# Scores of a gated recurrence in strips of 32 keys, and its values in native float32

## The chip, the cores and the metric

One core of a Trainium2 chip runs the whole program. The metric is the device time of one execution in microseconds; the time before is the median of three runs.

## What is computed

Two layers of a bidirectional encoder over 512 tokens of width 1024. Each layer mixes three branches (latent attention, a gated recurrence, windowed attention) by gates, then adds cross-attention and a SwiGLU block. The change concerns the recurrence, which for each of 8 heads is, forward and once more on reversed time:

```
b = cumsum(log_f)            # within chunks
scores = (q * exp(b)) @ (k * exp(-b)).T     # tril
o = scores @ v + (q * exp(b)) @ state
state = state * exp(b_last) + (k * exp(b_last - b)).T @ v
```

Each head has keys of 128 and values of 64 elements. The sum of both directions is normalized and gated.

## The kernel before

All activations stand transposed, features on the 128 partitions and the 512 tokens along the columns. Weights stream from HBM in 764 blocks of 128x512 float32. Each is split into a high part `whi` (L120, ScalarE, rounded to the reduced format float32r) and a low part `wlo` (L121, VectorE, the rest), and a projection is three matmuls in parts (`mm3`: high x high, high x low, low x high). All matmuls go through `mm` (L151). `split` (L180 on ScalarE, L181 on VectorE) makes such parts of activations.

The recurrence isn't computed as a scan over a state. `hgrn_decay` makes from the gates the decayed queries and keys of one head and direction, once for tokens within 32 (`qk`: forward queries and keys in 0 and 1, backward in 2 and 3), and for four levels of distance the factors `lf` (forward) and `lr` (backward): level 0 for neighbouring 32s, level 1 for neighbouring 64s, levels 2 and 3 for 128s and 256s. `hgrn_scores` then builds the full 512x512 table of scores of the head, keys on partitions, 128 keys at a time:

- bank `bd` gets, for each of the four 128-token blocks `j`, one 128x128 float32 matmul of the forward `qk`, and bank `bb` one of the backward `qk`; 24 small matmuls then overwrite the places in `bd` that lie across 32s and 64s;
- two predicated copies (L482) take the valid places of both banks to `zz`, whose other places stay zero from a memset at the start; an add (L484) sums them; ScalarE (L487) and VectorE (L488) write high and low part into the diagonal blocks of `ah` and `al`;
- eight wide float32 matmuls, in three banks `g`, fill the blocks off the diagonal, which `split` writes into `ah` and `al`.

The values of the head are 12 matmuls in parts of 512 columns (four blocks, three each); the token-major values `vs` come in parts from `vturn`, for two heads at once, and the half of the result that is the other head's is left unread. The loop in `hgrn` goes over 8 heads: scores of head i, projections of head i + 2, values of head i, decay of head i + 2. The order of instructions on each engine is made by the framework's scheduler, not by the source alone. TensorE runs through the projections meanwhile; the code draws buffers from the pools `c8` (14 of 128x2048 float32), `t2` (25 of 128x512) and 8 PSUM banks.

The layers' other parts are unchanged. The latent attention has a token-major copy of its values of its own (`vtoken`, float32 without parts) and multiplies them as half-width float32 matmuls: two heads side by side on the two halves of the array's columns.

Of the kernel before, what the change touches and what calls it, by code (L numbers as in the profile page):

```python
# [48 lines left out]
def _consts():  # L49
    c = np.zeros((P, CTOT), np.float32)  # L50
    inv = (10000.0 ** (-np.arange(16, dtype=np.float32) / np.float32(16))).astype(np.float32)
    ang = np.arange(T, dtype=np.float32)[:, None] * inv[None, :]
    cos = np.cos(ang).T.astype(np.float32)
    sin = np.sin(ang).T.astype(np.float32)
    cs = np.concatenate([cos, cos, -sin, sin], 0)
    one = np.ones((64, T), np.float32)
    rope = np.stack([np.concatenate([one, cs], 0), np.concatenate([cs, one], 0)])
    t = np.arange(T)
    c[:, C_M:C_M + T] = (t % 16 != 0)
    c[:, C_ID:C_ID + P] = np.eye(P)  # L60
    p = np.arange(P)
    c[:, C_SWAP:C_SWAP + P] = (p[:, None] == p[None, :]) | (p[:, None] == (p[None, :] ^ 32))
    c[:, C_BONE:C_BONE + P] = ((p[:, None] // 64) == (p[None, :] // 64))
    j = np.arange(16)
    for i in range(4):
        n = 1 << i
        c[:, C_SM + 16 * i:C_SM + 16 * i + 16] = (j % n != 0)
        c[:, C_SM + 64 + 16 * (3 - i):C_SM + 80 + 16 * (3 - i)] = (j % n != 0)
    same = (p[:, None] // 32) == (p[None, :] // 32)
    mf = (~same) | (p[:, None] <= p[None, :])  # L70
    mb = same & (p[:, None] >= p[None, :])
    m = np.concatenate([mf, mb], 1).astype(np.int32)
    return c, m, rope


class _K:
# [119 lines left out]
    def setup(self):  # L196
        nc = self.nc
        self.cst = self.tl("cst", [P, CTOT])
        nc.sync.dma_start(self.cst, self.cstd)
        self.ident = self.cst[:, C_ID:C_ID + P]  # L200
        nc.vector.memset(self.ones, 1.0)
        nc.vector.memset(self.eps, EPS)

        b = self.vec[:, V_LB:V_LB + 32].rearrange("p (d l h) -> p d l h", d=2, l=2)
        lbt = self.lbt
        v3 = lambda i: lbt[:, i].rearrange("p (d h) -> p d h", d=2)
        mx, e0, e1, s = v3(0), v3(1), v3(2), v3(3)
        tt = nc.vector.tensor_tensor
        tt(mx, b[:, :, 0], b[:, :, 1], op=ALU.max)
        tt(e0, b[:, :, 0], mx, op=ALU.subtract)  # L210
        tt(e1, b[:, :, 1], mx, op=ALU.subtract)
        nc.scalar.activation(lbt[:, 1:3], lbt[:, 1:3], AF.Exp)
        tt(s, e0, e1, op=ALU.add)
        nc.vector.reciprocal(lbt[:, 3], lbt[:, 3])
        tt(e0, e0, s, op=ALU.mult)
        tt(e1, e1, s, op=ALU.mult)
        tt(lbt[:, 4], lbt[:, 1], lbt[:, 1], op=ALU.subtract)
        tt(lbt[:, 5], lbt[:, 1], lbt[:, 2], op=ALU.add)
        tt(lbt[:, 5], lbt[:, 5], lbt[:, 1], op=ALU.subtract)
        nc.vector.tensor_scalar(lbt[:, 6:8], lbt[:, 4:6], -1.0, 1.0, op0=ALU.mult, op1=ALU.add)  # L220

        self.zz = self.tl("zz", [P, 2, 4, P])
        nc.gpsimd.memset(self.zz, 0.0)

    def col(self, c):
        return self.vec[:, c:c + 1]
# [53 lines left out]
    def vturn(self, vf):  # L280

        nc = self.nc
        tb = self.bank([P, 4, P])
        for j in range(4):
            nc.tensor.transpose(tb[:, j], vf[:, j * P:(j + 1) * P], self.ident)
        v = (self.t2(F32R, (P, 4, P)), self.t2(F32R, (P, 4, P)))
        self.split(v[0], v[1], tb)
        return v

    def hgrn(self, l, x, xg, acc):  # L290
# [48 lines left out]
        for i in range(8):  # L339
            pr = i // 2  # L340
            if i > 0:
                a = self.hgrn_scores(heads[i])
            if i % 2 == 0:
                osb = self.t2()
                if 0 < i < 6:
                    values(pr + 1)
            else:
                g = proj("g", pr)
                sg = self.t2()
                last = nc.scalar.activation(sg, g, AF.Sigmoid)  # L350
                if i == 7:
                    self.pin(last)
                nc.vector.tensor_tensor(sg, g, sg, op=ALU.mult)
            if i < 6:
                take_z(heads[i + 2], [proj("f", i + 2), proj("b", i + 2)])
            elif i == 6:
                pre = self.mla_pre(l, h)
                for nm in ("ckv0", "ckv1", "key"):
                    pre[nm]()
            else:  # L360
                for nm in ("cq0", "nckv", "cq1", "rope"):
                    pre[nm]()
            ob = self.bank()
            vh, vl = vs[pr]
            for j in range(4):
                s = slice(j * T, (j + 1) * T)
                self.mm3(ob, (vh[:, j], vl[:, j]), (a[0][:, s], a[1][:, s]), j == 0, j == 3)
            hf = slice(64 * (i % 2), 64 * (i % 2) + 64)
            nc.scalar.activation(osb[hf], ob[hf], AF.Copy)
            if i % 2 == 1:  # L370
                sq = self.t2()
                nc.scalar.activation(sq, osb, AF.Square)
            if i < 6:
                take_q(heads[i + 2], proj("q", i + 2))
                if i % 2 == 0:
                    vs[pr + 1] = self.vturn(st["vf"])
            elif i == 7:
                pre["cq2"]()
            if i % 2 == 1:
                ob = self.bank()  # L380
                self.mm(ob, self.cst[:, C_BONE:C_BONE + P], sq, True, True)
            if i < 6:
                decay(heads[i + 2])
            elif i == 7:
                pre["ncq"]()
            if i % 2 == 1:
                r = self.t2()
                self.rsqrt(r, ob, 64)
                nc.vector.scalar_tensor_tensor(r, osb, self.col(lv + V_GOUT), r, op0=ALU.mult, op1=ALU.mult)
                nc.vector.tensor_tensor(r, r, sg, op=ALU.mult)  # L390
                self.split(y[pr][0], y[pr][1], r)
# [68 lines left out]
    def hgrn_scores(self, hd):  # L460
# [2 lines left out]
        tt = nc.vector.tensor_tensor  # L463
        one = lambda o, a, b: self.mm(o, a, b, True, True)
        qk, lf, lr = hd["qk"], hd["lt", 0], hd["lt", 1]
        bd, bb = self.bank([P, 4, P]), self.bank([P, 4, P])
        for j in range(4):
            js = slice(j * P, (j + 1) * P)
            one(bd[:, j], qk[:, 1, js], qk[:, 0, js])
            one(bb[:, j], qk[:, 3, js], qk[:, 2, js])  # L470
        for j in range(4):
            one(bd[0:64, j, 64:128], lf[:, 1, 1, 64 * j:64 * j + 64], lf[:, 1, 0, 64 * j:64 * j + 64])
            one(bd[64:128, j, 0:64], lr[:, 1, 1, 64 * j:64 * j + 64], lr[:, 1, 0, 64 * j:64 * j + 64])
            for i in range(2):
                a, b = 64 * i, 64 * i + 32
                ps = slice(64 * j + 32 * i, 64 * j + 32 * i + 32)
                one(bd[a:a + 32, j, b:b + 32], lf[:, 0, 1, ps], lf[:, 0, 0, ps])
                one(bd[b:b + 32, j, a:a + 32], lr[:, 0, 1, ps], lr[:, 0, 0, ps])
        ah, al = self.c8([P, 4 * T], F32R), self.c8([P, 4 * T], F32R)
        z = self.zz  # L480
        for i, b in enumerate((bd, bb)):
            nc.vector.copy_predicated(z[:, i], self.msk[:, i].unsqueeze(1).to_broadcast([P, 4, P]), b)  # L482
        zd = self.t2(shape=(P, 4, P))
        tt(zd, z[:, 0], z[:, 1], op=ALU.add)  # L484
        dg = lambda a: bass.AP(a.tensor, a.offset, [list(a.ap[0]), [640, 4], [1, P]])
        dh, dl = dg(ah), dg(al)
        nc.scalar.activation(dh, zd, AF.Copy)  # L487
        tt(dl, zd, dh.bitcast(F32), op=ALU.subtract)  # L488
        h0, h1 = slice(0, P), slice(P, 2 * P)
        for i in range(3):  # L490
            g = self.bank()
# [7 lines left out]
            else:  # L499
                one(g[:, 0:128], lf[:, 2, 1, h1], lf[:, 2, 0, h1])  # L500
                one(g[:, 128:384], lr[:, 3, 1, h1], lr[:, 3, 0])
                one(g[:, 384:512], lr[:, 2, 1, h1], lr[:, 2, 0, h1])
            s = slice(i * 640 + 128, (i + 1) * 640)
            self.split(ah[:, s], al[:, s], g)
        return ah, al

    def branch(self, l, gate, wname, rows, y, h, merged, first):

# [81 lines left out]
    def mla(self, l):  # L590
# [56 lines left out]
                    nc.vector.tensor_copy(pt[:, :, js], tb)  # L647
            return pt

        def vtoken(vf):  # L650

            tb = self.bank([P, 4, P])
            for j in range(4):
                nc.tensor.transpose(tb[:, j], vf[:, j * P:(j + 1) * P], self.ident)
            v = self.t2(shape=(P, 4, P))
            nc.scalar.activation(v, tb, AF.Copy)
            return v

        def values(pr, v, pts):

            def run():
# [8 lines left out]
        self.fill()  # L670
        vf = keys(0)
        self.fill()
        v = vtoken(vf)
        cq = self.mst["n", "cq"]
        qt = query(0)
        self.fill()
# [2 lines left out]
        for hd in range(8):  # L679
# [10 lines left out]
            if e == 1:  # L690
                pend, pts = values(pr, v, pts), []
                if hd < 7:
                    v = vtoken(vf)
            if hd < 7:
                ps = scores(qt, 1 - e)
        return y, pend
# [449 lines left out]
```

## Time and profile before

| what | value |
| --- | --- |
| time, median of 3 runs | 2477.17 us (2470.8 to 2479.98) |
| the profiled execution's own time | 2471.43 us |
| its span | 2469.6 us |
| mean granted TensorE clock | 0.995 |
| TensorE / weight loads / VectorE / ScalarE / GpSimd busy | 98% / 81% / 63% / 49% / 11% |
| recurrence of layer 0, layer 1 in the trace | about 30 to 320 us, 1255 to 1545 us |

Busy time is that of instructions on an engine; a matmul's end is modelled, and matmuls overlap. L151 is line 151 of the kernel, where all matmuls are recorded, so their groups are told apart by tile and shape. 128*64 means 128 rows and 64 columns of the array.

### The profile page before, as it was taken

What the parts mean: (1) busy time and instruction counts of PE and PEld (TensorE: products, weight loads), DVE (VectorE), ACT (ScalarE), POOL (GpSimd) and SP (SyncE); (2) the same over time, 40 slices, a digit from 0 to 9 for tenths busy, and PEclk for the clock granted to TensorE, in tenths of its full rate; (3) what the DMA queues carried; (4) which work ended last, traced back from release to release, by engine and by line L of the source; (5) the groups of instructions that cost most, each with busy time, mean ns of one, the idle gap of its engine ahead of it and who ended that gap; (6) DMA issues with size and microseconds to landing.
All of it is one profiled execution on the core that took longest, in us unless ns stands there. A gap on an engine that the chain in (4) does not pass through costs nothing.

```text
span 2469.6 us, 32711 instructions
## 1 busy us (share of the span) xinstructions
PE 2422.0 (98%) x12038; PEld 1999.7 (81%) x12038; DVE 1545.8 (63%) x2787; ACT 1215.4 (49%) x2213; POOL 262.6 (11%) x197
## 2 busy tenths in 40 slices
PE   8999999999999999999998999999999999999998
PEld 6788877788888888888877887887888888888886
DVE  8888666676665655355577776766766656553553
ACT  7666565455554533233466665654554445332332
POOL 2455300000000000000035542000000000000000
PEclk9999999999999999999999999999999999999999
DMA  4211322223453333333421222221224523333332
GB/s 140 70 61 55 90 74 60 63 73 100 140 138 98 86 95 98 96 96 98 129 73 60 69 74 63 73 64 60 81 79 149 146 78 89 97 96 98 98 96 76
DMA packets 119681, 220.96 MB, mean 89 GB/s; under 512 B 13281, under 2 KB 15585, under 8 KB 119137
## 3 DMA queue, kind: packets, MB, share of 16 engines
q1 hardware_dynamic: 119520, 218.88, 30.1%
q8 instruction: 94, 1.54, 0.3%
q14 instruction: 67, 0.54, 0.1%
HBM read 214.63 MB, written 4.19 MB: 89 GB/s over the span
## 4 chain that ended last, share of the span: by engine, by line
PE 82%; DVE 8%; issue 4%; ACT 3%; POOL 2%; DMA 1%; SPq 0%; DVEq 0%; ACTq 0%; POOLq 0%
PE ps L151 80%; POOL t L404 2%; DVE c L457 1%; PE ps L643 1%; DVE smx L411 1%; ACT whi L120 1%; POOL t L408 1%; DVE c L439 1%; DVE t L411 1%; DVE wlo L121 1%; PE ps L787 0%; DVE c L438 0%; DVE zz L482 0%; DMA c<-in_memT_dram 0%; DVE t L434 0%
## 5 line engine op out<-in xcount | busy, mean ns | idle before, releaser
L151 PE MATMUL ps<-c,whi 128*128 128x512 f32 (+1 forms) x5696 | 1734.7, 386 | 6.2 <-ACT whi L120 6.0
L151 PEld LDWEIGHTS ps<-c,whi 128*128 128x128 f32 x5696 | 1061.0, 188 | 227.7 <-issue 10.8
L151 PE MATMUL ps<-c,wlo 128*128 128x512 f32 (+1 forms) x2848 | 1098.9, 386 | 15.3 <-DVE wlo L121 15.2
L120 ACT ACTIVATE whi<-wraw 128x512 fp32r<-128x512 f32 x764 | 475.2, 630 | 841.7 <-PE ps L151 621.6
L121 DVE TENSOR_TENSOR wlo<-wraw,whi 128x512 fp32r<-128x512 f32 x764 | 520.2, 690 | 533.9 <-ACT whi L120 516.6
L151 PEld LDWEIGHTS ps<-c,wlo 128*128 128x128 f32 x2848 | 536.4, 188 | 126.7 <-DVE wlo L121 20.2
L151 PE MATMUL ps<-c,t 128*128 128x512 f32 (+4 forms) x896 | 185.6, 386 | 4.3 <-DVE c L181 2.8
L404 POOL TENSOR_SCALAR t<-t 128x512 f32<-128x512 f32 x32 | 71.7, 2242 | 1081.2 <-ACT t L401 1079.7
L151 PEld LDWEIGHTS ps<-c,t 128*128 128x128 f32 (+2 forms) x896 | 133.9, 182 | 43.6 <-issue 16.9
L457 POOL TENSOR_TENSOR c<-c,smx 128x256 f32<-128x256 f32 x128 | 145.0, 1161 | 74.3 <-DVE c L438 64.3
L966 DVE TENSOR_TENSOR t<-ps,t 128x512 f32<-128x512 f32 x112 | 76.2, 688 | 103.1 <-PE ps L151 103.1
L180 ACT ACTIVATE c<-ps 128x512 fp32r<-128x512 f32 (+3 forms) x200 | 97.7, 527 | 84.1 <-PE ps L151 81.3
L181 DVE TENSOR_TENSOR c<-ps,c 128x512 fp32r<-128x512 f32 (+3 forms) x200 | 114.9, 598 | 28.5 <-ACT c L180 27.4
L151 PE MATMUL ps<-c 128*32 128x32 f32 (+3 forms) x1280 | 108.1, 255 | 5.5 <-DVE c L439 5.5
L151 PEld LDWEIGHTS ps<-c 128*32 128x32 f32 (+2 forms) x1280 | 94.9, 148 | 21.3 <-DVE c L439 4.0
L948 DVE TENSOR_TENSOR c<-ps,c 128x512 f32<-128x512 f32 x64 | 44.2, 690 | 73.0 <-PE ps L151 73.0
L457 DVE TENSOR_TENSOR c<-c,smx 128x256 f32<-128x256 f32 x128 | 67.7, 587 | 0.3
L181 DVE TENSOR_TENSOR c<-t,c 128x512 fp32r<-128x512 f32 (+1 forms) x84 | 51.9, 633 | 2.9 <-ACT c L180 2.9
L408 POOL TENSOR_TENSOR t<-t,t 128x512 f32<-128x512 f32 x32 | 44.7, 1397 | 84.1 <-ACT t L407 84.1
L180 ACT ACTIVATE c<-t 128x512 fp32r<-128x512 f32 (+1 forms) x84 | 47.8, 581 | 9.4 <-DVE t L390 3.3
L406 ACT ACTIVATE t<-t 128x512 f32<-128x512 f32 x32 | 20.1, 629 | 62.4 <-POOL t L404 62.4
L411 DVE TENSOR_TENSOR_SCAN t<-cst,t 128x512 f32<-128x512 f32 x32 | 40.8, 1275 | 15.8 <-POOL t L408 15.8
(144 smaller groups left out, 1888.7 us busy)
## 6 DMA issues: line engine op xcount, KB each, us to landing
wraw<-in_w_dram SPq DMA_DIRECT2D x764, 256.0 KB, 2.7
c<-in_xT_dram SPq DMA_DIRECT2D x16, 256.0 KB, 5.1
t<-in_bias_dram SPq DMA_DIRECT2D x16, 192.0 KB, 2.8
c<-in_memT_dram SPq DMA_DIRECT2D x3, 1024.0 KB, 8.0
xs<-c SPq DMA_DIRECT2D x8, 256.0 KB, 2.4
c<-xs SPq DMA_DIRECT2D x8, 256.0 KB, 4.3
out_dram<-t SPq DMA_DIRECT2D x8, 256.0 KB, 2.0
t<-in_rope_dram SPq DMA_DIRECT2D x4, 256.0 KB, 3.1
```

The lines of the kernel that those rows point to most:

```text
L120: self.nc.scalar.activation(hi, raw, AF.Copy)
L121: self.nc.vector.tensor_tensor(lo, raw, hi.bitcast(F32), op=ALU.subtract)
L151: self.nc.tensor.matmul(o, a, b, start=start, stop=stop)
L180: nc.scalar.activation(hi, src, AF.Copy)
L181: nc.vector.tensor_tensor(lo, src, hi.bitcast(F32), op=ALU.subtract)
L404: nc.gpsimd.tensor_scalar(g, f, TINY, KNEE, op0=ALU.max, op1=ALU.min)
L408: nc.gpsimd.tensor_tensor(f, f, g, op=ALU.add)
L411: scan = lambda o, m, x: nc.vector.tensor_tensor_scan(o, m, x, 0.0, op0=ALU.mult, op1=ALU.add)
L439: nc.vector.scalar_tensor_tensor(ki, kk, omlb, cc, op0=ALU.mult, op1=ALU.mult)
L457: eng.tensor_tensor(ov, sv, ev, op=ALU.mult)
L948: nc.vector.tensor_tensor(x[c], b, xold[c], op=ALU.add)
L966: self.nc.vector.tensor_tensor(t, b, r, op=ALU.mult)
```

## The change

`hgrn_scores` computes the scores within 128 tokens as strips: 32 keys at a time on one quarter of the array's columns, for the forward 32s, the backward 32s, the level-0 and the level-1 neighbours, four strips in a row on the four quarters. The backward scores need 32 columns a bank row instead of 128. There are no parts any more: one copy of the diagonal blocks, four adds on 32 partitions each for the backward places, one copy for each bank `g`. `vturn` returns float32 values, and the values of a head are four float32 matmuls on its own half of the columns. `vtoken` was the same as the new `vturn` and goes.

```
-    mb = same & (p[:, None] >= p[None, :])
+    mb = (p[:, None] % 32) >= p[None, :]
...
-        self.zz = self.tl("zz", [P, 2, 4, P])
-        nc.gpsimd.memset(self.zz, 0.0)
+        zz = self.tl("zz", [P, 8, P])
+        nc.gpsimd.memset(zz, 0.0)
+        self.zz, self.zb = zz[:, 0:4], zz[:, 4].rearrange("p (a b) -> p a b", a=4)
...
-        v = (self.t2(F32R, (P, 4, P)), self.t2(F32R, (P, 4, P)))
-        self.split(v[0], v[1], tb)
+        v = self.t2(shape=(P, 4, P))
+        nc.scalar.activation(v, tb, AF.Copy)
...
-            vh, vl = vs[pr]
+            hf = slice(64 * (i % 2), 64 * (i % 2) + 64)
             for j in range(4):
-                s = slice(j * T, (j + 1) * T)
-                self.mm3(ob, (vh[:, j], vl[:, j]), (a[0][:, s], a[1][:, s]), j == 0, j == 3)
-            hf = slice(64 * (i % 2), 64 * (i % 2) + 64)
+                self.mm(ob[hf], vs[pr][:, j, hf], a[:, j * T:(j + 1) * T], j == 0, j == 3)
...
-        bd, bb = self.bank([P, 4, P]), self.bank([P, 4, P])
+        bd, bb = self.bank([P, 4, P]), self.bank([P, 4, 32])
+        q4 = [slice(32 * g, 32 * g + 32) for g in range(4)]
         for j in range(4):
-            js = slice(j * P, (j + 1) * P)
-            one(bd[:, j], qk[:, 1, js], qk[:, 0, js])
-            one(bb[:, j], qk[:, 3, js], qk[:, 2, js])
-        for j in range(4):
-            one(bd[0:64, j, 64:128], lf[:, 1, 1, 64 * j:64 * j + 64], lf[:, 1, 0, 64 * j:64 * j + 64])
-            one(bd[64:128, j, 0:64], lr[:, 1, 1, 64 * j:64 * j + 64], lr[:, 1, 0, 64 * j:64 * j + 64])
-            for i in range(2):
-                a, b = 64 * i, 64 * i + 32
-                ps = slice(64 * j + 32 * i, 64 * j + 32 * i + 32)
-                one(bd[a:a + 32, j, b:b + 32], lf[:, 0, 1, ps], lf[:, 0, 0, ps])
-                one(bd[b:b + 32, j, a:a + 32], lr[:, 0, 1, ps], lr[:, 0, 0, ps])
-        ah, al = self.c8([P, 4 * T], F32R), self.c8([P, 4 * T], F32R)
-        z = self.zz
-        for i, b in enumerate((bd, bb)):
-            nc.vector.copy_predicated(z[:, i], self.msk[:, i].unsqueeze(1).to_broadcast([P, 4, P]), b)
-        zd = self.t2(shape=(P, 4, P))
-        tt(zd, z[:, 0], z[:, 1], op=ALU.add)
-        dg = lambda a: bass.AP(a.tensor, a.offset, [list(a.ap[0]), [640, 4], [1, P]])
-        dh, dl = dg(ah), dg(al)
-        nc.scalar.activation(dh, zd, AF.Copy)
-        tt(dl, zd, dh.bitcast(F32), op=ALU.subtract)
+            js = [slice(j * P + 32 * g, j * P + 32 * g + 32) for g in range(4)]
+            for g in range(4):
+                one(bd[q4[g], j, q4[g]], qk[:, 1, js[g]], qk[:, 0, js[g]])
+            for g in range(4):
+                one(bb[q4[g], j], qk[:, 3, js[g]], qk[:, 2, js[g]])
+            for g in range(4):
+                ps = slice(64 * j + 32 * (g // 2), 64 * j + 32 * (g // 2) + 32)
+                lt = lf if g % 2 == 0 else lr
+                one(bd[q4[g], j, q4[g ^ 1]], lt[:, 0, 1, ps], lt[:, 0, 0, ps])
+            for g in range(4):
+                ks = slice(64 * j + 32 * (g % 2), 64 * j + 32 * (g % 2) + 32)
+                lt = lf if g < 2 else lr
+                cs = slice(64, 128) if g < 2 else slice(0, 64)
+                one(bd[q4[g], j, cs], lt[:, 1, 1, ks], lt[:, 1, 0, 64 * j:64 * j + 64])
+        a = self.c8([P, 4 * T])
+        nc.vector.copy_predicated(self.zz, self.msk[:, 0].unsqueeze(1).to_broadcast([P, 4, P]), bd)
+        nc.vector.copy_predicated(self.zb, self.msk[:, 1, 0:32].unsqueeze(1).to_broadcast([P, 4, 32]), bb)
+        dg = bass.AP(a.tensor, a.offset, [list(a.ap[0]), [640, 4], [1, P]])
+        nc.scalar.activation(dg, self.zz, AF.Copy)
+        for g in range(4):
+            tt(dg[q4[g], :, q4[g]], self.zz[q4[g], :, q4[g]], self.zb[q4[g]], op=ALU.add)
...
-            s = slice(i * 640 + 128, (i + 1) * 640)
-            self.split(ah[:, s], al[:, s], g)
-        return ah, al
+            nc.scalar.activation(a[:, i * 640 + 128:(i + 1) * 640], g, AF.Copy)
+        return a
```

## Rows read from the trace of the kernel before

**Rows 1.** The page: span, and each engine's busy us, share, instructions.

```profile
span 2469.6 us, 32711 instructions
...
PE 2422.0 (98%) x12038; PEld 1999.7 (81%) x12038; DVE 1545.8 (63%) x2787; ACT 1215.4 (49%) x2213; POOL 262.6 (11%) x197
```

**Rows 2.** Busy time by stage: length, PE, PEld, DVE, ACT, POOL, clock, DMA, GB/s.

```profile
30.00:320.00 290.00, 276.89 (x1602) 226.41 (x1601) 221.60 (x404) 183.19 (x308) 130.05 (x96) 0.99 0.23 69
...
620.00:1255.00 635.00, 634.93 (x2946) 530.15 (x2945) 347.44 (x565) 257.59 (x452) 0.00 (x0) 1.00 0.37 107
1255.00:1545.00 290.00, 276.17 (x1595) 225.11 (x1594) 218.62 (x399) 180.75 (x306) 131.37 (x96) 0.98 0.22 68
```

**Rows 3.** Waits of TensorE, 30 to 320 us: total, times, longest.

```profile
PE ps L151 <- DVE wlo L121: 5.8, 4, 2.3
...
PE ps L151 <- DVE c L181: 1.7, 1, 1.7
```

**Rows 4.** Waits of TensorE, 1255 to 1545 us.

```profile
PE ps L151 <- DVE wlo L121: 9.4, 6, 3.7
...
PE ps L151 <- DVE c L181: 1.0, 1, 1.0
```

**Rows 5.** TensorE alone by stretch, one head's scores: length, busy (count), clock, DMA, GB/s.

```profile
123.09:124.96 1.87, 1.87 (x17) 1.00 0.67 149
124.96:126.82 1.86, 1.86 (x49) 1.00 0.37 134
126.82:129.46 2.64, 2.64 (x24) 1.00 0.00 0
...
125.23:125.43 0.20, 0.20 (x12) 1.00 0.89 328
```

**Rows 6.** Timeline of TensorE, one head's values: start, us, instructions.

```profile
147.42 2.88 PE L151 MATMUL ps<-c,t 128*128 128x512 f32 x12
150.14 0.61 PE L151 MATMUL ps<-c,whi 128*128 128x512 f32 x2
```

**Rows 7.** Timeline of TensorE, one pair of attention values and its neighbours.

```profile
375.30 0.39 PE L151 MATMUL ps<-t,wlo 128*128 128x512 f32 x1
375.62 3.65 PE L151 MATMUL ps<-c,t 128*64 128x512 f32 x16
379.20 0.73 PE L151 MATMUL ps<-c,whi 128*128 128x512 f32 x2
```

**Rows 8.** Groups of VectorE instructions, 30 to 320 us: busy, mean ns, idle before.

```profile
L181 DVE TENSOR_TENSOR c<-ps,c 128x512 fp32r<-128x512 f32 x24 | 15.4, 678 | 0.2 <-ACT c L180 0.2
...
L482 DVE COPY_PREDICATED zz<-msk,ps 128x512 f32<-128x512 int32 x16 | 11.7, 735 | 2.6 <-PE ps L151 2.6
...
L434 DVE TENSOR_TENSOR t<-t,smx 128x256 f32<-128x256 f32 x16 | 6.7, 418 | 0.0
L488 DVE TENSOR_TENSOR c<-t,c 128x512 fp32r<-128x512 f32 x8 | 6.6, 831 | 0.0
...
L484 DVE TENSOR_TENSOR t<-zz 128x512 f32<-128x512 f32 x8 | 5.5, 681 | 0.1
...
L425 DVE TENSOR_TENSOR smx<-smx,t 128x64 f32<-128x64 f32 x16 | 4.3, 270 | 0.1
```

**Rows 9.** Timeline of VectorE ahead of a wait of TensorE.

```profile
143.68 0.68 DVE L484 TENSOR_TENSOR t<-zz 128x512 f32<-128x512 f32 x1
144.29 0.68 DVE L121 TENSOR_TENSOR wlo<-wraw,whi 128x512 fp32r<-128x512 f32 x1
```

**Rows 10.** Timeline of TensorE at that wait; in brackets idle and releaser.

```profile
143.16 0.61 PE L151 MATMUL ps<-c,whi 128*128 128x512 f32 x2
145.02 0.50 PE L151 MATMUL ps<-c,wlo 128*128 128x512 f32 x1 [1.24 <-DVE wlo L121]
```

**Rows 11.** Busy time by stretch around a fall of the clock, as rows 2.

```profile
105.40:108.00 2.60, 0.33 (x2) 0.00 (x0) 2.60 (x10) 1.22 (x3) 0.16 (x1) 1.00 0.00 0
108.70:112.00 3.30, 3.30 (x10) 2.49 (x8) 3.27 (x5) 3.29 (x7) 3.25 (x4) 0.50 0.30 79
```

More of the change, by code (lines that the diff above doesn't have):

```diff
@@ L648, in turned @@
             return pt
[L650 to L657, printed above, removed]
         def values(pr, v, pts):
@@ L672, in mla @@
         self.fill()
-        v = vtoken(vf)
+        v = self.vturn(vf)
         cq = self.mst["n", "cq"]
@@ L692, in mla @@
                 if hd < 7:
-                    v = vtoken(vf)
+                    v = self.vturn(vf)
             if hd < 7:
```

## The prediction

> **What bounds the kernel now.** Read first the busy time of each engine over the span: TensorE is busy 2422.0 of 2469.6 us, VectorE 1545.8, ScalarE 1215.4 [rows 1]. So there is hardly a stretch where TensorE could be filled better, and a change pays mainly by making TensorE's own work shorter. Next the same view by stage. The two stretches with the recurrence (30 to 320 us and 1255 to 1545 us) are where TensorE is idle: 290.00 - 276.89 = 13.1 us in the first, 13.8 us in the second; between 620 and 1255 us it is idle for 0.1 us of 635 [rows 2]. In those two stretches VectorE is busy 221.6 and 218.6 of 290 us, three quarters of the time. The view of waits says who was late: the low part of a streamed weight block (`wlo`, L121, a VectorE subtraction) in 4 waits of 5.8 us together in the first stretch and 6 waits of 9.4 us in the second, and the low part of the scores (`c`, L181) in 1.7 and 1.0 us [rows 3, 4]. VectorE is late there, and a TensorE matmul stands behind it. The change edits this stage alone: 8 heads in each of 2 layers, 16 calls of `hgrn_scores`.
>
> **TensorE, scores within 128 tokens.** Now: eight 128x128 float32 matmuls, then 24 small ones. The trace has two MATMUL records for each float32 matmul, so 16 and 48. They take 1.87 and 1.86 us, together 3.73 us a head [rows 5]; a count in these rows includes the records still in flight at its start. (The eight wide matmuls behind them, 2.64 us [rows 5], stay.) New: 16 rounds of four strip matmuls, 32 keys on each quarter of the columns, 12 rounds with 32 queries streamed and 4 with 64; together 64 matmuls, 128 records. No row shows rounds back to back, so I bound them.
>
> Low end: a 128-column record takes 1.87/16 = 0.117 us. A strip loads and streams a quarter of the columns: estimate 0.029 us, and two records in a row on each quarter make a round of 0.058 us, or 0.117 us with 64 queries. Per 128 tokens 3 x 0.058 + 0.117 = 0.29 us, times 4 = 1.17 us. A change of the array's shape costs about 0.09 us: before the attention values the last wide matmul begins at 375.30 and would be followed 0.227 us later (three matmuls of this kind take 0.68 us: 12 in 2.72 [rows 6]), but the first half-width one begins at 375.62 [rows 7]. In and out: 0.18 us. Sum 1.35 us.
>
> High end: four strips with their eight records took 0.20 us, 125.23 to 125.43, to the next shape [rows 5]; they run side by side, or they would take longer than a full 128-column pair. Sixteen such rounds and 4 x 0.058 for the wider ones: 3.43, with 0.09 on the way in 3.5 us.
>
> I take the row that is nearest, four strips, less the change of shape that is in it: 0.20 - 0.09 = 0.11 us a round; 16 x 0.11 + 0.23 + 0.18 = 2.2 us. That saves 3.73 - 2.2 = 1.5 us a head; between 2.4 and 0.2 by the bounds.
>
> The Trainium skill, "TensorE: Matmul & The Clock Gate", section "Back-to-back issue gap", speaks against this: it gives a matmul of 1 to 64 columns a floor of some 60 cycles, about 25 ns, and by that the estimate for 128 records is 3.2 us. The rows neither show nor exclude it: eight records in 0.20 us are 25 ns each, but with the change of shape in them.
>
> **TensorE, values.** Now 12 matmuls of 512 columns in parts, from 147.42 to 150.14: 2.72 us [rows 6]. New: four float32 matmuls, eight records, on 64 columns. The attention values are the same form: 16 records, two halves of the array side by side, run from 375.62 to 379.20, 3.58 us [rows 7]. Here one half is empty, so eight records take as long as those sixteen. With 0.09 us into the shape, and the pair of wide matmuls behind it taking 0.73 instead of 0.62 us, it is 3.78 us: 1.06 us more a head. This term is sure to 0.1 us. The move from parts to native float32 is a loss on TensorE; it is VectorE that gains by it.
>
> TensorE together: -1.5 + 1.06 = -0.47 us a head, -7.5 us for 16; by the bounds -21 to +13 us. Since TensorE is busy almost throughout, I count it in full.
>
> **VectorE.** Per head go: the add L484 (0.681), the subtraction L488 (0.831) and three subtractions at L181 from PSUM (0.678 each) [rows 8]. The second predicated copy (L482, 0.735) shrinks from 512 to 128 columns. Four adds on 32 partitions and 128 columns come; 64 columns cost 0.270 and 256 cost 0.418 [rows 8], so I take 0.31 each, and the same for the short copy. Old 4.28, new 5 x 0.31 = 1.55 us: 2.7 us a head, 43 us in all; the token turn of the values loses its subtraction too. ScalarE keeps its copies, one for each it had.
>
> This is worth only what TensorE waits. Look at one wait: the weight matmul of 143.16 is followed at 145.02, 1.24 us idle, released by L121 [rows 10]; VectorE did the add L484 from 143.68 and only then L121 from 144.29 [rows 9]. Without L484 (0.6 us from start to start) and with the second copy 0.4 us shorter earlier in this chain, L121 comes 1.0 us sooner and 0.2 us of wait is left. Ten such waits hold 15.2 us, two more 2.7 us [rows 3, 4]: at most 18 us, and about 12 us at 1.0 us each. I take 7.5 us. The framework's scheduler orders VectorE anew, one of the four adds can land where L484 was, and a TensorE that is faster by 0.5 us a head comes to the same weight block earlier. What is late next is the decay of the following head, which fills VectorE ahead of L121 and stays. Nothing is counted for the clock: the granted clock was 0.50, the level of 1.2 GHz, from 108.70 to 112.00, right behind 2.60 us in which TensorE was busy for 0.33 [rows 11]; shorter waits there could give back up to half of these 3.3 us.
>
> **Edits costed at nothing.** The memset has the same 1024 columns, at the start, under loading. `zz` and `zb` are read by ScalarE and the four adds until the next head's copies, some 30 us later. One `c8` buffer a head instead of two and one `t2` for the values only free memory. No DMA moves; weights flow as before. The adds wait for ScalarE's copy of the diagonal, since both write it; behind a waiting add on VectorE stand L121 and the next decay. The copy itself no longer waits for L484, so I expect no new stall. If it comes, each costs up to 0.6 us, one ScalarE copy.
>
> **Sum.** -7.5 (TensorE) - 7.5 (waits) = -15 us. The profiled execution took 2471.4 us, so 2456 us in its own terms; it lies 5.7 us under the median of three, 2477.2, whose runs spread over 9 us. In terms of the median: 2462 us.
>
> **Rivals.**
> 1. The strips run at the pace of their columns (1.35 us a block). For it: the four side by side in 0.20 us with a change of shape. Then -21 - 7.5 = -28.5: 2449 us.
> 2. Every record costs 25 ns however narrow, block 3.5 us. The row of four strips has just this pace; against it, the change of shape is inside. Then +13 - 7.5 = +5.5: 2483 us. The floor of the Trainium skill, above, would give a block close to this one.
> 3. Slower: TensorE hands out small records no faster than in the 24 small matmuls, 48 in 1.86 us, 39 ns each. Then the block takes 4.96 us, each head 1.23 + 1.06 = 2.3 us more, +36.6 - 7.5 = +29: 2506 us. It decides beyond half a per cent from 31 ns a record on (block 3.9 us). Against it: seven changes of shape lie in those 1.86 us.
> 4. TensorE as I say, but VectorE's new order keeps L121 as late as it is: -7.5 alone, 2470 us.
>
> **How the numbers follow.** Chances: forecast 0.42, its own range 2453 to 2471; rival 1 0.20, rival 2 0.20, rival 3 0.10, rival 4 0.08. What this kernel's measurement can tell from no change is about half a per cent, 12.4 us, so faster means under 2464.8. Of the forecast 0.26 lies under that and 0.16 over it. Faster: 0.26 + 0.20 = 0.46. Same: 0.16, rival 4 and nearly all of rival 2: 0.42. Slower: rival 3 and the rest, 0.12. A range of 2443 to 2488 us leaves out rival 3 and the outer part of rival 1, some 0.16.
>
> **What would show it.** Right: a head's strip block of 128 records in 2.0 to 2.5 us between the last 128-column projection and the first wide score matmul; eight half-width records of about 0.43 us apart for the values; VectorE some 45 us less busy; waits on L121 in these two stretches down from 15.2 to about half. Wrong: a block over 3 us (rivals 2 and 3) or under 1.6 us (rival 1); waits at the old sum, or a new one on the four adds or on the values' matmuls.

## The result, and the profile after

The changed kernel is 1.1% slower: 2505.24 us median (2502.49 to 2506.14) against 2478.27 us for the kernel before on the same chip, a ratio of 1.0113 [1.009, 1.0135]. Forecast were 2462 us, in a range of 2443 to 2488 us. One execution further down, the profiled one of e8, was disturbed (8207.31 us, where its other six took 2462.73 to 2466.68), and what e8 waits for is read from e12, the same kernel.

The page of the kernel after: span and busy time, beside [rows 1].

```profile
span 2502.9 us, 34617 instructions
...
PE 2419.5 (97%) x12998; PEld 1955.0 (78%) x12998; DVE 1517.1 (61%) x2763; ACT 1220.2 (49%) x2217; POOL 237.8 (10%) x197
```

TensorE is idle for 2502.9 - 2419.5 = 83.4 us; before it was 2469.6 - 2422.0 = 47.6 us. Its busy time hardly fell, but work takes nearly twice the busy time at half the clock (three matmuls of a weight block 1.28 us, 219.53 to 220.81 in the trace after, where they take 0.68 at full clock). The mean granted clock went from 0.995 to 0.987, so the loss to the clock, span times one minus clock, is some 12.3 us before and 32.5 us after (the third digit leaves 1.2 us open in each). What remains is work at full clock: 2422.0 - 12.3 = 2409.7 before, 2419.5 - 32.5 = 2387.0 after. So the 33.3 us of longer span are **-22.7 work, +35.8 idle, +20.2 clock**. This split is used for all runs below. It is a rough one: a part of the low clock falls in the waits themselves, so it books somewhat too much as clock and too little as work. It also holds for one execution of each kernel, and that of before took 2471.43 us, below its median; by the medians the change costs 27.0 us and not 33.3.

Busy time by stage after, as [rows 2]; the two recurrences are now the first and last row.

```profile
30.00:335.00 305.00, 274.27 (x2075) 203.02 (x2074) 205.88 (x391) 184.37 (x308) 118.43 (x96) 0.95 0.21 66
...
620.00:1260.00 640.00, 639.93 (x2977) 534.56 (x2976) 346.61 (x566) 259.00 (x459) 0.00 (x0) 1.00 0.36 109
1260.00:1580.00 320.00, 287.76 (x2131) 213.31 (x2130) 216.16 (x408) 192.28 (x323) 118.25 (x96) 0.96 0.20 63
```

All of it is in the recurrence: 30.7 and 32.2 us idle where it was 13.1 and 13.8, and the clock 0.95 and 0.96 where it was 0.99 and 0.98. Who is waited for, first recurrence and then second, beside [rows 3, 4]:

```profile
PE ps L151 <- DVE wlo L121: 16.8, 4, 5.6
PE ps L151 <- DVE c L489: 7.9, 3, 3.5
...
PE ps L151 <- DVE wlo L121: 19.4, 6, 5.5
PE ps L151 <- DVE c L489: 7.9, 3, 3.5
```

Waits on L121 rose from 15.2 to 36.2 us, with as many waits; new are 15.8 us for the four adds (L489).

**TensorE's own work did fall.** One head's strips after, beside the first two rows of [rows 5], TensorE alone:

```profile
122.83:124.23 1.40, 1.40 (x129) 1.00 0.00 1
```

The block takes 1.40 us where it took 3.73. The values after, beside [rows 6]:

```profile
75.40 0.39 PE L151 MATMUL ps<-c,wlo 128*128 128x512 f32 x1
75.72 3.65 PE L151 MATMUL ps<-c,t 128*64 128x512 f32 x8
79.30 0.73 PE L151 MATMUL ps<-c,whi 128*128 128x512 f32 x2
```

From 75.72 to 79.30 they take 3.58 us where it was 2.72. With the two changes of shape (0.32 us from the last wide matmul into it where 0.23 is usual, and 0.73 for the next pair where 0.62 is) it is 3.78, as forecast. Together -2.33 + 1.06 = -1.27 us a head, -20 us for 16 heads: that is the -22.7 above, within what its rounding leaves open.

**Where it went: a wait of 5.57 us.** It is in the fifth head. TensorE, then VectorE, then GpSimd at this place of the kernel after:

```profile
211.48 0.61 PE L151 MATMUL ps<-c,whi 128*128 128x512 f32 x2
217.66 0.79 PE L151 MATMUL ps<-c,wlo 128*128 128x512 f32 x1 [5.57 <-DVE wlo L121]
```

```profile
199.91 0.75 DVE L484 COPY_PREDICATED zz<-msk,ps 128x512 f32<-128x512 int32 x1
...
211.48 1.10 DVE L389 TENSOR_TENSOR t<-t,t 128x512 f32<-128x512 f32 x1
212.51 2.68 DVE L456 TENSOR_TENSOR c<-c,smx 128x256 f32<-128x256 f32 x4
...
215.72 1.17 DVE L489 TENSOR_TENSOR c<-zz 32x128 f32<-32x128 f32 x4
216.92 3.10 DVE L121 TENSOR_TENSOR wlo<-wraw,whi 128x512 fp32r<-128x512 f32 x5
```

```profile
211.07 3.51 POOL L456 TENSOR_TENSOR c<-c,smx 128x256 f32<-128x256 f32 x4 [1.57 <-ACT whi L120]
```

The same head in the kernel before, in the same order:

```profile
210.05 0.50 PE L151 MATMUL ps<-c,wlo 128*128 128x512 f32 x1 [1.16 <-DVE wlo L121]
```

```profile
194.45 0.75 DVE L482 COPY_PREDICATED zz<-msk,ps 128x512 f32<-128x512 int32 x1
...
206.77 1.42 DVE L457 TENSOR_TENSOR c<-c,smx 128x256 f32<-128x256 f32 x4
...
208.71 0.68 DVE L484 TENSOR_TENSOR t<-zz 128x512 f32<-128x512 f32 x1
209.31 0.68 DVE L121 TENSOR_TENSOR wlo<-wraw,whi 128x512 fp32r<-128x512 f32 x1
```

```profile
205.75 6.90 POOL L457 TENSOR_TENSOR c<-c,smx 128x256 f32<-128x256 f32 x4 [1.70 <-DVE c L438]
```

The chain on VectorE is the same: the predicated copy, the decay of the next head, the gated output of the last pair of heads (L390 before, L389 after), the add or adds, L121. From the copy to L121 it took 209.31 - 194.45 = 14.86 us and now takes 216.92 - 199.91 = 17.01, though one copy has left it: of the rows shown, the four multiplies (L457, now L456) take 1.26 us longer, and the four adds 0.49 us longer than the one add. The wait grew by 5.57 - 1.16 = 4.41 us: 2.15 from this chain, and the other 2.26 is TensorE, which arrives sooner by nearly the 2.33 that the score block lost.

At the place of [rows 9, 10], the third head, on which the forecast worked out its term, VectorE and TensorE after:

```profile
128.98 0.75 DVE L484 COPY_PREDICATED zz<-msk,ps 128x512 f32<-128x512 int32 x1
...
144.78 0.68 DVE L121 TENSOR_TENSOR wlo<-wraw,whi 128x512 fp32r<-128x512 f32 x1
```

```profile
145.51 0.80 PE L151 MATMUL ps<-c,wlo 128*128 128x512 f32 x1 [4.29 <-DVE wlo L121]
```

Here the adds stand behind this L121, and the chain is still 15.80 us long. Before, the copy began at 129.39, so it was 144.29 - 129.39 = 14.90: L121 comes 0.90 us later in the chain, not 1.0 us sooner, and the wait is 4.29 instead of 1.24 us.

Behind the wait of 5.57 us the clock falls, as in [rows 11]:

```profile
212.10:217.60 5.50, 0.00 (x0) 0.00 (x0) 5.43 (x12) 5.36 (x10) 2.48 (x3) 0.91 0.00 0
218.00:223.40 5.40, 5.40 (x12) 3.32 (x12) 2.71 (x5) 1.67 (x4) 0.00 (x0) 0.50 0.73 243
```

The second kind of wait is in the second, fourth and sixth head: the values stand ready and wait for the adds, which VectorE runs behind the same multiplies of the decay. TensorE, then VectorE:

```profile
181.93 5.32 PE L151 MATMUL ps<-c,t 128*64 128x512 f32 x8 [2.21 <-DVE c L489]
```

```profile
178.00 2.69 DVE L456 TENSOR_TENSOR c<-c,smx 128x256 f32<-128x256 f32 x4
180.61 1.16 DVE L489 TENSOR_TENSOR c<-zz 32x128 f32<-32x128 f32 x4
```

### The profile page after: what moved, and what is told of

Same layout as the page of the kernel before. It is cut to its first block, busy times and chain, and to the rows that moved or that the text cites. A ratio compares the mean times of both kernels' runs of the same rounds, so it can differ in the third digit from the quotient of the medians.

```text
span 2502.9 us, 34617 instructions
## 1 busy us (share of the span) xinstructions
PE 2419.5 (97%) x12998; PEld 1955.0 (78%) x12998; DVE 1517.1 (61%) x2763; ACT 1220.2 (49%) x2217; POOL 237.8 (10%) x197
## 4 chain that ended last, share of the span: by engine, by line
PE 79%; DVE 10%; issue 4%; ACT 4%; POOL 3%; DMA 0%; SPq 0%; DVEq 0%; POOLq 0%; ACTq 0%
PE ps L151 77%; DVE c L456 2%; POOL t L403 2%; PE ps L643 1%; DVE smx L410 1%; DVE wlo L121 1%; DVE c L438 1%; DVE t L410 1%; POOL t L407 1%; ACT whi L120 1%; DVE smx L428 1%; DVE c L437 1%; PE ps L778 0%; DVE t L433 0%; DVE c L489 0%
## 5 line engine op out<-in xcount | busy, mean ns | idle before, releaser
L151 PE MATMUL ps<-c,wlo 128*128 128x512 f32 (+1 forms) x2848 | 1102.7, 387 | 36.3 <-DVE wlo L121 36.2
L120 ACT ACTIVATE whi<-wraw 128x512 fp32r<-128x512 f32 x764 | 476.9, 630 | 878.2 <-PE ps L151 655.4
L121 DVE TENSOR_TENSOR wlo<-wraw,whi 128x512 fp32r<-128x512 f32 x764 | 524.5, 695 | 580.5 <-ACT whi L120 559.8
L151 PE MATMUL ps<-c,t 128*64 128x512 f32 (+4 forms) x832 | 202.3, 426 | 17.2 <-DVE c L489 15.8
L151 PEld LDWEIGHTS ps<-c,t 128*128 128x128 f32 (+2 forms) x832 | 115.5, 175 | 87.7 <-issue 48.1
L456 POOL TENSOR_TENSOR c<-c,smx 128x256 f32<-128x256 f32 x128 | 118.5, 955 | 77.0 <-DVE c L437 58.8
L180 ACT ACTIVATE c<-ps 128x256 fp32r<-128x256 f32 (+3 forms) x152 | 72.1, 507 | 71.0 <-PE ps L151 68.6
L181 DVE TENSOR_TENSOR c<-ps,c 128x256 fp32r<-128x256 f32 (+3 forms) x152 | 84.1, 574 | 32.6 <-ACT c L180 31.6
L151 PEld LDWEIGHTS ps<-c 128*32 128x32 f32 (+1 forms) x2304 | 64.9, 124 | 22.0 <-issue 8.0
L151 PE MATMUL ps<-c 128*32 128x32 f32 (+3 forms) x2304 | 74.1, 223 | 7.9 <-DVE c L438 6.3
L456 DVE TENSOR_TENSOR c<-c,smx 128x256 f32<-128x256 f32 x128 | 75.1, 645 | 0.2
L405 ACT ACTIVATE t<-t 128x512 f32<-128x512 f32 x32 | 20.2, 630 | 62.9 <-POOL t L403 62.9
L151 PE MATMUL ps<-t,whi 128*128 128x512 f32 x160 | 49.5, 390 | 0.0
```

The lines of the kernel that those rows point to most:

```text
L120: self.nc.scalar.activation(hi, raw, AF.Copy)
L121: self.nc.vector.tensor_tensor(lo, raw, hi.bitcast(F32), op=ALU.subtract)
L151: self.nc.tensor.matmul(o, a, b, start=start, stop=stop)
L180: nc.scalar.activation(hi, src, AF.Copy)
L181: nc.vector.tensor_tensor(lo, src, hi.bitcast(F32), op=ALU.subtract)
L456: eng.tensor_tensor(ov, sv, ev, op=ALU.mult)
```

## The experiments

Each time is a median, each ratio is to the kernel before on the same chip with its 95% interval; idle and clock are worked out as above from each run's span, TensorE busy time and mean granted clock. The kernel before had medians of 2475.93 to 2479.93 us in its four sets of runs, so a difference between two rows is good to about 4 us.

| run | us | ratio | idle | clock | L121 waits |
| --- | --- | --- | --- | --- | --- |
| before (profiled 2471.4) | 2478.3 | | 47.6 | 12 | 15.2 |
| after | 2505.2 | 1.0113 [1.009, 1.0135] | 83.4 | 33 | 36.2 |
| e1 padded | 2494.4 | 1.0063 [1.0044, 1.0083] | 54.9 | 20 | 23.3 |
| e2 no adds | 2477.7 | 1.0001 [0.9989, 1.0013] | 63.9 | 25 | 31.3 |
| e3 parts earlier | 2506.0 | 1.0108 [1.0087, 1.0128] | 83.1 | 35 | 35.7 |
| e4 scores first | 2436.3 | 0.9829 [0.981, 0.9848] | 36.3 | 10 | 2.6 |
| e5 before, scores first | 2493.5 | 1.0063 [1.0042, 1.0085] | 61.9 | 22 | 2.8 |
| e6 strips only | 2529.9 | 1.0207 [1.0185, 1.0229] | 118.6 | 56 | 82.4 |
| e7 values only | 2488.8 | 1.0034 [1.0021, 1.0047] | 48.7 | 17 | 20.9 |
| e8 strips only, scores first | 2463.7 | 0.9942 [0.9926, 0.9958] | | | |
| e9 scores first, padded | 2482.8 | 1.0019 [1.0003, 1.0036] | 50.4 | 17 | 21.1 |
| e10 scores first, no adds | 2435.2 | 0.9835 [0.982, 0.9849] | 34.0 | 10 | 3.2 |
| e11 values only, scores first | 2463.4 | 0.9949 [0.9934, 0.9963] | 31.1 | 7 | 3.3 |
| e12 as e8, for its trace | 2466.0 | 0.9954 [0.994, 0.9968] | 70.4 | 25 | 14.6 |

**e1, more work for TensorE.** Eight matmuls into a bank that nothing reads, in each head:

```
+        pad = self.bank([P, 4, P])
+        for _ in range(2):
+            for j in range(4):
+                js = slice(j * P, (j + 1) * P)
+                one(pad[:, j], qk[:, 1, js], qk[:, 0, js])
```

> The changed kernel with eight more 128x128 float32 matmuls in every head's score block, into a bank that nobody reads: some 1.9 us more TensorE work a head, 30 us in all, at the place where the strips saved it. Theory A (what the strips and values save on TensorE is not lost there, but turns into waiting: TensorE now comes early to a weight block whose low part, L121, stands behind the next head's decay in VectorE's order): the time stays within 10 us of the changed kernel's 2505, since the waits on L121 and on the adds L489 shrink by about what is added. Theory B (the strips or the half-width values themselves cost the time): 2535 us.

Sixteen records of 0.117 us are 1.87 us a head [rows 5], 30 us in all, and the kernel became 10.8 us faster: 0.8 us outside theory A's range, and 41 us from theory B's time. TensorE and VectorE at the place of the 5.57 us:

```profile
214.06 0.50 PE L151 MATMUL ps<-c,wlo 128*128 128x512 f32 x1 [3.77 <-DVE wlo L121]
```

```profile
208.91 2.69 DVE L456 TENSOR_TENSOR c<-c,smx 128x256 f32<-128x256 f32 x4
...
212.12 1.16 DVE L494 TENSOR_TENSOR c<-zz 32x128 f32<-32x128 f32 x4
213.31 3.10 DVE L121 TENSOR_TENSOR wlo<-wraw,whi 128x512 fp32r<-128x512 f32 x5
```

VectorE's order here is unchanged, and the wait is shorter by 5.57 - 3.77 = 1.80 us, what the padding takes. So at this wait TensorE's shorter block had bought nothing: what it saved it waited, one for one. Over the kernel the waits on L121 fall from 36.2 to 23.3 us and those on the adds (L494 here) from 15.8 to 0.7, 28.0 us together for some 30 us of added work, and the clock gives back some 12.

**e2, without the four adds.**

```
-        for g in range(4):
-            tt(dg[q4[g], :, q4[g]], self.zz[q4[g], :, q4[g]], self.zb[q4[g]], op=ALU.add)
```

> The changed kernel without the four narrow adds L489, so without the backward scores within 32 tokens. Theory C (the adds are the new cost: narrow instructions on VectorE, and TensorE's values waiting for them): back to the kernel before or below it, under 2480 us. Theory A: the adds are 1.2 us of a chain of 17 us; the waits on L489 go (16 us in the trace), but the weight blocks behind the decay are only 1.2 us earlier each; 2485 to 2497 us, waits on L121 still over 25 us.

Theory A's range is missed, theory C's number is met: 27.6 us less than after. The 15.8 us of waits on L489 go, L121 waits 4.9 us less, and the clock gives back some 8. So the four adds, 1.17 us of VectorE's time a head, cost 1.7 us a head. Of the 36.2 us for L121, 31.3 stay.

**e3, weights taken apart earlier.** How many weight blocks ahead L120 and L121 are issued:

```
-LOOK = 3
+LOOK = 4
```

> The changed kernel with the weight parts made one 512-column unit earlier (LOOK 4 instead of 3): VectorE gets L121 some 2.7 us of TensorE work sooner. Theory A: the ten waits on L121 of 36 us lose up to 2.7 us each, and the clock falls less often; 2475 to 2490 us. Theory C (adds): the waits on L489 stay and the time moves by less than 8 us. If the time doesn't move at all, the order of L121 against the decay is not the cause.

No change, and theory A's gain missed. By the expectation's last sentence that speaks against the order as the cause. But the edit didn't move the order. VectorE of e3 at the place of the 5.57 us:

```profile
201.85 0.75 DVE L484 COPY_PREDICATED zz<-msk,ps 128x512 f32<-128x512 int32 x1
...
218.85 3.10 DVE L121 TENSOR_TENSOR wlo<-wraw,whi 128x512 fp32r<-128x512 f32 x5
```

From the copy to L121 it is 17.00 us, where it was 17.01, and the wait is 5.56: one block more of lookahead in the code leaves L121 where it stood, behind the decay. So e3 says nothing for or against the order.

**e4, scores of the next head ahead of the decay.** In the loop over heads:

```
-            if i > 0:
-                a = self.hgrn_scores(heads[i])
...
+            if i < 7:
+                a = self.hgrn_scores(heads[i + 1])
             if i < 6:
                 decay(heads[i + 2])
```

> The changed kernel with each head's scores issued ahead of the decay of the head after it, instead of behind it; the same work. VectorE's order then has the adds and several L121 between the pieces of the decay. Theory A: waits on L489 nearly go (16 us to under 4) and those on L121 halve; 2450 to 2475 us, under the kernel before, since the TensorE work that was saved (some 22 us) can then be had. Theory B: no better than 2495 us.

The whole loss is gone and 42 us of the time before with it, 14 us more than theory A's best. VectorE, ahead of the place where TensorE waited:

```profile
127.32 1.17 DVE L489 TENSOR_TENSOR c<-zz 32x128 f32<-32x128 f32 x4 [0.52 <-ACT c L487]
...
135.81 0.66 DVE L121 TENSOR_TENSOR wlo<-wraw,whi 128x512 fp32r<-128x512 f32 x1
...
140.22 1.12 DVE L121 TENSOR_TENSOR wlo<-wraw,whi 128x512 fp32r<-128x512 f32 x1
141.26 2.68 DVE L456 TENSOR_TENSOR c<-c,smx 128x256 f32<-128x256 f32 x4
```

The adds come in the middle of the decay, and L121 is let in ahead of its last multiplies. The multiplies themselves take as long as after at this place, and longer over the whole kernel (87.3 us for VectorE's 128, against 75.1); VectorE is as busy (1514.0 us). No wait on L489 is left, and 2.6 us on L121. The same work in another order is worth 69 us. The edit moves the scores on every engine, so this is the worth of the whole order and not of VectorE's alone.

**e5, the same move in the kernel before.** The diff is that of e4 on the old code.

> The kernel before, with each head's scores issued ahead of the decay of the head after it: the same move as in the run with scores first, without the change. Theory A (order on VectorE and the change are two things that add up): it wins what the kernel before waits for VectorE and the slow clock behind it, 10 to 20 us: 2458 to 2468 us, so that in this order the change is worth 20 to 30 us. Theory D (the order only mends what the change broke): 2478 us, within 6.

Both forecasts missed: some 15 us slower. L121 waits do fall, to 2.8 us, but TensorE waits 26.5 us in six waits on ScalarE's square for the norm (L370). ScalarE and TensorE at one of 6.01 us (the longest is 7.3):

```profile
110.83 1.28 ACT L435 ACT_TABLE_LOAD   x1 [3.38 <-DVE t L434]
...
121.89 0.61 ACT L370 ACTIVATE t<-t 128x512 f32<-128x512 f32 x1
```

```profile
122.56 2.07 PE L151 MATMUL ps<-t,cst 128*128 128x512 f32 x2 [6.01 <-ACT t L370]
```

ScalarE stands 3.38 us for what the decay's exponents are made from on VectorE (L434). The square is in its order behind that and behind the 11 us of other work that follow. e11 below takes the parts of scores and values away, and with them this wait. So the order alone isn't the gain either.

**e6, strips alone; e7, native values alone.** e6 is the changed kernel with the parts kept (and so one more copy of the diagonal, the adds on it and the subtraction of its low part); e7 keeps the new float32 values and scores with the old full-width matmuls, banks and the single add. Cuts of both edits, against the kernel after:

```
-        a = self.c8([P, 4 * T])
+        ah, al = self.c8([P, 4 * T], F32R), self.c8([P, 4 * T], F32R)
...
+        dh, dl = dg(ah), dg(al)
+        nc.scalar.activation(dh, zd, AF.Copy)
+        tt(dl, zd, dh.bitcast(F32), op=ALU.subtract)
```

```
-        nc.scalar.activation(dg, self.zz, AF.Copy)
-        for g in range(4):
-            tt(dg[q4[g], :, q4[g]], self.zz[q4[g], :, q4[g]], self.zb[q4[g]], op=ALU.add)
+        tt(dg, z[:, 0], z[:, 1], op=ALU.add)
```

> The kernel before with the scores within 128 tokens in strips, the scores and values still in parts (one more copy on ScalarE, the four narrow adds, and the subtraction of the low part as before). TensorE does 2.3 us a head less, 37 us in all. Theory A: nothing of it is had, waits take it and the narrow adds lie in the chain: 2470 to 2510 us. If strips are a plain gain: 2441 us.

> The changed kernel with the old score block (full 128x128 matmuls, both copies, one add of 512 columns straight into the float32 scores): only the values and scores without parts are left of the change. TensorE does 0.86 us a head more (14 us), VectorE four subtractions a head less. Theory A: the waits on VectorE shrink a little, 2478 to 2492 us. If the lighter VectorE were what pays: under 2470 us.

e6 is the slowest kernel of all, outside its range: the strips save TensorE's time in front of a VectorE that has more to do than before, and 82.4 us of waits on L121 follow, the longest 11.4. e7 is in its range, though not by waits that shrink, as its expectation had it. It isolates the prediction's VectorE term: VectorE is busy 1514.2 us, 31.6 less than before, and yet the waits on L121 in the profiled executions are 20.9 instead of 15.2 us. VectorE and TensorE of e7 at the place of [rows 9, 10]:

```profile
128.53 0.74 DVE L480 COPY_PREDICATED zz<-msk,ps 128x512 f32<-128x512 int32 x1
...
141.12 2.69 DVE L455 TENSOR_TENSOR c<-c,smx 128x256 f32<-128x256 f32 x4
...
144.34 0.68 DVE L482 TENSOR_TENSOR c<-zz 128x512 f32<-128x512 f32 x1
144.94 3.08 DVE L121 TENSOR_TENSOR wlo<-wraw,whi 128x512 fp32r<-128x512 f32 x5
```

```profile
145.67 0.50 PE L151 MATMUL ps<-c,wlo 128*128 128x512 f32 x1 [2.71 <-DVE wlo L121]
```

From the copy to L121 it is 16.41 us, 1.51 longer than before, and the wait is 2.71 - 1.24 = 1.47 longer. The other add (0.6 us) still stands there, and the decay's multiplies take 2.69 instead of 1.42.

The medians are milder. TensorE's work in e7 is (2441.0 - 17.4) - 2409.7 = 13.9 us more than before, but its time is only 8.9 us longer (2488.78 against 2479.93 on the same chip; 5 to 12 us by the interval). So waits and clock together are some 5 us shorter in the medians, where they are 6 us longer in the profiled executions. That of e7 took 2491.5 us, above its median, that of before 2471.43, below its own.

**e8, e12, strips alone with the scores first; e11, native values alone with the scores first.** The edits of e6 and e7 together with that of e4. e12 is the kernel of e8 once more, for its trace.

> Strips with the values still in parts, and scores issued ahead of the decay. TensorE does the least of all versions (the values cost 2.72 instead of 3.58 us a head, 14 us in all, against the run with scores first), VectorE the most in this order. If VectorE's work can hide in this order: 2422 us. If VectorE's four more subtractions a head bring the waits back: 2436 to 2450 us, and then native float32 values are worth their TensorE time.

> The kernel of e8 once more, for a trace: strips, values and scores still in parts, scores first; 2464 us. Order theory: no long waits for L121 behind the decay; what it loses to e4 (28 us) are waits for ScalarE, which has one copy more of the diagonal and stands behind VectorE, as in e5. Rival: the same waits for L121 as in e6, fewer.

> Old score block of full-width matmuls, native float32 scores and values, scores issued ahead of the decay: the last corner beside before with that order (2494), strips with parts and that order (2464) and e4 (2436). Theory that native values and scores are what lightens VectorE and ScalarE enough for that order: TensorE is the bound as in e4 and only the longer block is added, 2.3 us for 16 heads, 37 us: 2466 to 2476 us. Rival (that order makes ScalarE late by itself, as it did in the kernel before): 2482 to 2496 us.

e8 missed both its ranges; e12 shows why it isn't as fast as e4. It waits 16.5 us on ScalarE's square (L371 there), as e5 does, but 14.6 us on L121 as well, which the order theory had left out. The execution traced took 2473.4 us, above its median. e11 came out 3 us under the range of the first theory and far from the rival: with native values there is no wait on ScalarE's square at all. Against e4 it is 2463.4 - 2436.3 = 27 us slower: some 35 us more work by the split, for the longer score block, less 5 us of idle time and 2 of clock. So in this order each half of the change pays, with or without the other: the strips 30 us (e5 to e8) and 27 us (e11 to e4), the native values 30 us (e5 to e11) and 27 us (e8 to e4). That the parts cost on ScalarE and VectorE is read from the waits of e5 and e12.

**e9, the padding of e1 on e4; e10, e4 without the adds.**

> The kernel of e4 (changed kernel, scores issued ahead of the decay) with the eight further matmuls of e1 in each head's score block, into a bank that nothing reads. Order theory (in the changed kernel TensorE waits because VectorE has the four adds and L121 behind the next head's decay; with the scores first TensorE is the bound again): the same matmuls that made the changed kernel 11 us faster now cost their full time, some 28 us, so 2461 to 2468 us against 2436, with the waits for L121 still under 5 us. Rival (a fuller TensorE is good by itself, since its clock falls behind gaps): 2430 to 2445 us.

> The kernel of e4 without the four adds of L489; it leaves out the backward scores within 32 tokens. Order theory: the adds cost 27 us in the changed kernel only because of what they stood behind; with the scores first they are hidden, so 2430 to 2438 us, within 0.3% of e4. Rival (the adds cost by their own time on VectorE, 1.17 us a head and more, whatever the order): 2410 to 2422 us.

e10 is as expected: the adds that cost 27.6 us in the old order cost 1 us in this one, too little to tell from nothing. e9 has the sign that was expected, but missed its range and its bound on the waits: it costs 46 us where 28 were expected, some 30 of work, and waits on L121 of 21.1 instead of 2.6 us with the clock behind them. VectorE of e9 ahead of such a wait:

```profile
141.45 2.68 DVE L456 TENSOR_TENSOR c<-c,smx 128x256 f32<-128x256 f32 x4
...
144.66 2.48 DVE L121 TENSOR_TENSOR wlo<-wraw,whi 128x512 fp32r<-128x512 f32 x4
```

With eight matmuls more in the program the scheduler put L121 behind the multiplies again, where e4 has it in front. The order that e4 gets isn't secured by anything in the code.

## Why the prediction was wrong

**The step that failed** is the worth of the waits: "L121 comes 1.0 us sooner and 0.2 us of wait is left", then "I take 7.5 us". VectorE's work before L121 was counted, as if what leaves the engine left the chain to L121. At the very place of that sentence L121 came 0.90 us later in the chain and the wait was 4.29 us; in the fifth head the chain grew by 2.15 us, and in the third by 1.51 us with the native values alone (e7), where VectorE lost 31.6 us of work. Instead of 7.5 us fewer, the waits on L121 became 21.0 us more. (Whether the lighter VectorE alone gains something is open: the profiled executions of before and e7 say no, their medians leave some 5 us.)

With it falls "I count it in full" for TensorE's own gain. The forecast had only named, not priced, what came beside it: "a TensorE that is faster by 0.5 us a head comes to the same weight block earlier". It was faster by 1.27 us a head, by 2.33 in the score block ahead of the weight block, and e1 shows that where TensorE waits such time is waited in full. So the two gains, counted apart and added, were not to be had together.

**The adds**: "I expect no new stall. If it comes, each costs up to 0.6 us, one ScalarE copy." It came as 15.8 us of waits, up to 3.5 us each, because the adds stand behind the next head's decay and not behind the copy. With what they cost on L121 and the clock it is 27.6 us (e2), and 1 us where they stand well (e10).

**The clock**: "Nothing is counted for the clock" was wrong by some 20 us. It follows from the two steps above: longer waits, and behind the one shown a stretch at 0.50.

**Strips**: the term of 2.2 us a block was mis-sized; it measured 1.40 us, which is rival 1's pace. **Values**: 3.78 us, right. **VectorE**: 28.7 us lighter, not 43. The adds were 0.281 us each, near the 0.31 taken, but two other groups grew; the decay's multiplies on VectorE and the gating of the output in the kernel before, and then after:

```profile
L457 DVE TENSOR_TENSOR c<-c,smx 128x256 f32<-128x256 f32 x128 | 67.7, 587 | 0.3
L390 DVE TENSOR_TENSOR t<-t,t 128x512 f32<-128x512 f32 x8 | 5.4, 677 | 0.0
```

```profile
L456 DVE TENSOR_TENSOR c<-c,smx 128x256 f32<-128x256 f32 x128 | 75.1, 645 | 0.2
L389 DVE TENSOR_TENSOR t<-t,t 128x512 f32<-128x512 f32 x8 | 8.0, 999 | 0.0
```

That is 10 of the 14 us.

Of the rivals, the third gave nearly the measured time (2506 us) by a mechanism that is disproved. The fourth was nearest in mechanism, but held the waits at their old sum; that they grow when TensorE gets faster was in no case. What stays open: why the multiplies became slower on VectorE, and why the scheduler puts L121 ahead of them in e4 and behind them in e9. Only the resulting orders were read, not its choices. Nor was it tried to fix the order by hand.

## What to carry to other kernels

Where TensorE waited for another engine here, work taken from TensorE ahead of that wait was worth nothing, and relief of the other engine can be worth only what leaves the chain up to the instruction that is waited for. So read that chain's order first, from its last common point to the releaser, and ask what stands ahead of it that nobody waits for. Padding TensorE is a cheap test of this: if the kernel doesn't get slower, its work isn't what bounds there. Look whether the order of the other engines stayed as it was: it did at the place read in e1, and in e9 it didn't. A change that loses may be right and stand in the wrong order: the same strips and values gave 1.0113 with the next head's decay issued first and 0.9829 with the scores first.

## What the hardware showed that was not expected

**Narrow matmuls.** 128 records of 32 and 64 columns on the four column quarters took 1.40 us, 11 ns each. Less the forecast's 0.18 us for the changes of shape that is 1.22 us for 20 times 32 columns on all quarters, 0.061 us each; the low estimate of 0.058 had that pace. The floor of 25 ns a matmul that the Trainium skill gives ("TensorE: Matmul & The Clock Gate", "Back-to-back issue gap") is not seen here: by it the block would have taken 3.2 us.

**VectorE and GpSimd side by side.** The decay's multiplies run on both at the same time. In the fifth head, before the change VectorE took 1.42 us for its four and GpSimd 6.90; after it 2.68 and 3.51 (GpSimd's spans are rough in these traces). The same instructions were slow on one engine or on the other. The Trainium skill ("SBUF — State Buffer", "Who interferes with whom") says that a VectorE instruction with two inputs from SBUF contends with GpSimd's reads, and that the order of issue decides which of them blocks. The two traces agree with the contention, but no run here took GpSimd's multiplies away to show it. What decides isn't seen in them: GpSimd's four begin first in both, 1.02 us ahead of VectorE's before the change and 1.44 us after it.
